# Two-term products of an MLP's up projection: from fp32r parts to scaled f16 parts

## The chip, the core and the metric

The kernel runs on one core of one Trainium2 chip. The metric is device time in microseconds (us): from the start to the end of one execution. Three runs of the kernel before took 3511.21, 3514.76 and 3516.85 us, and its time is their median, 3514.76 us.

The engines are named as in the profile: PE is TensorE (matmuls), PEld its weight loads, DVE is VectorE, ACT is ScalarE, POOL is GpSimd and SP is SyncE, which here only issues DMAs.

## The reference

One layer of a backbone over 2048 latent tokens of width 1024 and 256 context tokens. A projection feeds two mixers side by side, softmax attention (8 query heads, 2 key heads) and a gated delta rule (4 heads, both directions, in chunks of 64). Their outputs are projected and added; then comes a gated MLP with a convolution of width 3 over the positions:

```
x = x + g1 * lat_out
x = x + g2 * conv_ffn(modulate(x, norm2_g, sh2, sc2), w_up, ffn_conv_w, ffn_conv_b, w_down)
return rms_norm(x, final_norm_g)

def modulate(x, g, shift, scale):
    return rms_norm(x, g) * (1.0 + scale) + shift

def conv_ffn(h, w_up, conv_w, conv_b, w_down):
    u = depthwise_conv(h @ w_up, conv_w) + conv_b
    gate, val = jnp.split(u, 2, axis=-1)
    return (jax.nn.silu(gate) * val) @ w_down
```

All of it is float32. `w_up` is 1024 x 5632, `w_down` 2816 x 1024.

## The kernel before, in words

**Products in two parts.** A float32 operand a is kept as a rounded part hi and a rest lo = a - hi. A product of two such operands is three matmuls into one PSUM tile: hi x hi, hi x lo and lo x hi (`prods`, L512 to L521, one line for each). In the projections both parts are fp32r; in the attention both are f16.

**Stages.** Times are those of the profiled execution.

- 0 to 280 us: norm of the input, modulation terms, q, k, v and z projections.
- 280 to 718 us: the delta rule's projections (`pg`), convolution, SiLU (`y`, L1022), normalised k with its decay (`kd`, L966 and L969), written to DRAM as `gsc` (L971). At its end the modulation terms for the MLP are put together (`mod2`, `aff2`, L1063 to L1066).
- 718 to 1780 us: the attention and the delta rule, interleaved (below).
- 1780 to 2027 us: output norms, output projection (`po`), residual, the norm ahead of the MLP. That norm's output h2 goes to DRAM (`h2c`).
- 2027 to 3514 us: the MLP, in four blocks of 512 tokens.

**What sets the order in the attention stage.** The two mixers are recorded as operations of five tracks: `a` (attention), `i0` and `i1` (the part of a chunk of each direction that needs no state), `d0` and `d1` (the part that needs it). A planner (`Plan.order`) gives each operation a duration by a formula, and an urgency by its track's weight, and lays them out engine by engine: on each engine the most urgent operation among those that could start within a short patience is next. The planned order is then issued as it is (`Plan.issue`, L398 to L403, so nearly all instructions of the stage carry L403). Every engine and every DMA queue works through its own list in that order. Tile buffers are rings with a fixed count (`RINGS`): a load into a ring waits until the last reader of the buffer is done.

In the attention a step takes two key chunks for the 4 heads of one key head: four score matmuls `sc`, exp on ACT (`p`), its f16 part `hp` (on DVE for 3 of 9 steps, on ACT for the other 6), the rest `lp` on POOL, and the products with the values (`ops`). There are 288 such steps. For the next group of heads the row maxima are formed ahead, from score tiles `sm` that DVE reduces (`mx`). The scores have one ring of two banks (ring `s` is 1). In the delta rule, `tT`, `tk` and `rows` are loaded for each chunk; `at` is a decay product of the chunk, made in track `i` and used in track `d`.

**The MLP.** For each block there are 44 units of the up projection and then 24 units of the down projection. A unit of the up projection is one block of 1024 x 128 weights: loaded on SP's queue (`fetch`), its hi part cast on ACT (`leading`, L1685), its rest on DVE (`rest`, L1690), 24 matmuls (`pu`). The parts are made two units ahead and the load is asked for four units ahead. `after_up` copies the result from PSUM on ACT (`ue`, L1716), applies the three taps of the convolution on DVE (L1724, L1727; they come from the columns C_FC to C_FB of the constant tile `cols`), and for every second unit forms SiLU(gate) * value in two fp32r parts (`hid`). The next block's h2 is loaded and split while the down projection runs (L1825, L1826).

## Time and profile before

| | |
|---|---|
| median of three runs | 3514.76 us |
| the profiled execution, in all | 3515.73 us |
| its span, first to last instruction | 3513.9 us |
| mean granted clock of TensorE | 0.980 |
| PE busy | 3355.6 us (95%) |
| DVE busy | 2298.6 us (65%) |
| ACT busy | 1639.6 us (47%) |
| POOL busy | 1410.7 us (40%) |
| DMA, whole span | 381.30 MB, mean 109 GB/s |
| `pu` matmuls, three lines | 550.5 + 549.0 + 548.5 us of rows |

The rows of a matmul overlap: a `pu` row lasts 391 ns in the mean, but the next one starts sooner. The pace is therefore read from starts, not from durations, and a busy PE is not a PE at its best pace. An engine's share over the whole span is a mean over stages with different limits; the windows by stage tell which engine is full where. "idle before" in a group is the time that the engine had nothing to do just ahead of those instructions, with what ended it.

### The profile page before, as it was taken

The page shows a single profiled execution, that of the slowest core. Times are in us where ns is not written, and L with a number is a line of the kernel's source. Part 1 is how long each engine was busy: PE and PEld are TensorE (multiplying, and loading weights), DVE is VectorE, ACT ScalarE, POOL GpSimd, SP SyncE. Part 2 cuts the span into 40 slices and gives each one's busy share as a digit, 9 for nine tenths or more (in the row PEclk, how much of TensorE's full clock was granted, in tenths as well). Part 3 has the DMA queues.
Part 4 walks back from the last instruction along what each step waited for, and adds up shares of the span by engine and source line. Part 5 has one row for each costly group of instructions (what it writes and reads, how often), then busy time and mean ns, then how long its engine had stood idle before and what let it go on. Part 6 is the DMA issues. An engine that isn't in the chain of part 4 may idle for free.

```text
span 3513.9 us, 65298 instructions
## 1 busy us (share of the span) xinstructions
PE 3355.6 (95%) x26281; PEld 2715.5 (77%) x26281; DVE 2298.6 (65%) x3619; ACT 1639.6 (47%) x2556; POOL 1410.7 (40%) x1423
## 2 busy tenths in 40 slices
PE   6799999979999999999978999999999999999998
PEld 3799878857777777777756778888888888888898
DVE  5665577887777777777655567735773476447743
ACT  4443233447777676777644443323332333224331
POOL 4684455437767777777765411100110010001100
PEclk7899999989999999999989999999999999999999
DMA  6323335651111222220146643343334333433332
GB/s 227 90 66 97 120 116 149 189 153 48 60 63 55 66 63 70 66 65 29 53 145 218 218 159 96 95 130 112 120 97 124 115 116 97 125 114 120 96 108 91
DMA packets 209199, 381.30 MB, mean 109 GB/s; under 512 B 20360, under 2 KB 95720, under 8 KB 208624
## 3 DMA queue, kind: packets, MB, share of 16 engines
q1 hardware_dynamic: 207056, 371.74, 33.4%
q0 software_dynamic: 1840, 5.39, 0.6%
q8 instruction: 206, 3.38, 0.4%
q14 instruction: 97, 0.79, 0.1%
HBM read 297.73 MB, written 79.72 MB: 107 GB/s over the span
## 4 chain that ended last, share of the span: by engine, by line
PE 77%; DVE 8%; POOL 6%; DMA 4%; issue 3%; ACT 2%; SPq 0%; POOLq 0%; DVEq 0%; ACTq 0%
PE pu L520 9%; PE pu L519 9%; PE pu L521 9%; PE sc L403 6%; PE ops L403 5%; PE pdn L521 5%; PE pdn L520 5%; PE pdn L519 5%; PE po L403 3%; PE sm L403 3%; PE pa L403 1%; PE pg L520 1%; PE pg L519 1%; PE pg L521 1%; PE pkk L403 1%
## 5 line engine op out<-in xcount | busy, mean ns | idle before, releaser
L403 POOL TENSOR_TENSOR lp<-p,hp 128x1024 f16<-128x1024 f32 x288 | 616.0, 2146 | 232.8 <-DVE hp L403 88.0
L519 PE MATMUL pu<-h,ws_u 128*128 128x512 f32 x1408 | 550.5, 391 | 2.8 <-ACT h L403 2.8
L520 PE MATMUL pu<-h,ws_u 128*128 128x512 f32 x1408 | 549.0, 390 | 2.5 <-DVE h L403 2.5
L521 PE MATMUL pu<-h,ws_u 128*128 128x512 f32 x1408 | 548.5, 390 | 0.0
L403 DVE TENSOR_REDUCE mx<-sm 128x1 f32<-128x512 f32 x512 | 336.1, 681 | 74.7 <-PE sm L403 72.6
L1718 POOL COPY carry<-ue 128x2 f32<-128x2 f32 x132 | 24.8, 188 | 891.4 <-ACT ue L1716 891.4
L403 ACT ACTIVATE p<-sc 128x1024 f32<-128x1024 f32 x288 | 294.9, 1024 | 182.7 <-PE sc L403 173.3
L519 PEld LDWEIGHTS pu<-h,ws_u 128*128 128x128 f32 x1408 | 264.7, 188 | 60.1 <-ACT h L403 4.8
L520 PEld LDWEIGHTS pu<-h,ws_u 128*128 128x128 f32 x1408 | 264.6, 188 | 59.6 <-DVE h L403 4.2
L521 PE MATMUL pdn<-hid,ws_d 128*128 128x512 f32 (+2 forms) x880 | 307.4, 349 | 0.0
L520 PE MATMUL pdn<-hid,ws_d 128*128 128x512 f32 (+2 forms) x880 | 307.4, 349 | 0.0
L521 PEld LDWEIGHTS pu<-h,ws_u 128*128 128x128 f32 x1408 | 264.8, 188 | 54.9
L519 PE MATMUL pdn<-hid,ws_d 128*128 128x512 f32 (+2 forms) x880 | 306.4, 348 | 0.0
L1727 DVE SCALAR_TENSOR_TENSOR cv<-ue,cols,cv 128x512 f32<-128x512 f32 (+1 forms) x352 | 264.9, 752 | 15.8 <-DVE cv L1724 0.5
L1716 ACT COPY ue<-pu 128x512 f32<-128x512 f32 x176 | 103.2, 586 | 367.6 <-PE pu L521 367.0
L1690 DVE TENSOR_TENSOR ws_u<-raw_u,ws_u 128x1024 fp32r<-128x1024 f32 x176 | 214.5, 1219 | 19.1 <-ACT ws_u L1685 19.1
L403 PE MATMUL sc<-q,kh 128*128 128x512 f16 x576 | 218.7, 380 | 4.5 <-ACT p L403 3.9
L1724 DVE TENSOR_SCALAR cv<-ue,cols 128x512 f32<-128x512 f32 (+1 forms) x176 | 96.3, 547 | 188.3 <-ACT ue L1716 183.3
L403 PE MATMUL sc<-qx,kx 128*128 128x512 f16 x576 | 218.6, 380 | 0.0
L1715 POOL COPY ue<-carry 128x2 f32<-128x2 f32 x176 | 95.4, 543 | 291.6 <-DVE cv L1727 291.3
L1690 DVE TENSOR_TENSOR ws_d<-raw_d,ws_d 128x1024 fp32r<-128x1024 f32 (+1 forms) x96 | 109.0, 1136 | 157.8 <-ACT ws_d L1685 155.6
L403 ACT CAST hp<-p 128x1024 f16<-128x1024 f32 x192 | 200.8, 1047 | 3.3
(580 smaller groups left out, 8068.1 us busy)
## 6 DMA issues: line engine op xcount, KB each, us to landing
raw_u<-in_wu SPq DMA_DIRECT2D x176, 512.0 KB
raw_d<-in_wd SPq DMA_DIRECT2D x64, 512.0 KB
tk<-gsc SPq DMA_DIRECT2D x34, 512.0 KB
tT<-gsc SPq DMA_DIRECT2D x66, 256.0 KB
wm<-in_wm SPq DMA_DIRECT2D x64, 256.0 KB
gsc<-kd SPq DMA_DIRECT2D x64, 256.0 KB
raw_o<-in_wo SPq DMA_DIRECT2D x32, 512.0 KB
raw_d<-in_wd SPq DMA_DIRECT2D x32, 384.0 KB
```

What stands on the lines that cost most here:

```text
L403: fn(**{k: v.get() if isinstance(v, Lazy) else v for k, v in kw.items()})
L519: PE.matmul(out=ps, lhsT=hi_l(k), rhs=hi_r(k), start=st, stop=False)
L520: PE.matmul(out=ps, lhsT=hi_l(k), rhs=lo_r(k), start=False, stop=False)
L521: PE.matmul(out=ps, lhsT=lo_l(k), rhs=hi_r(k), start=False, stop=en)
L1690: V.tensor_tensor(out=made[u][:, 1, :n], in0=raws[u][:, :n], in1=made[u][:, 0, :n].bitcast(F32), op=ALU.subtract)
L1715: G.tensor_copy(out=ue[:, 0:2], in_=carry[:, b, :])
L1716: S.copy(out=ue[:, 2:514], in_=ps)
L1718: G.tensor_copy(out=carry[:, b, :], in_=ue[:, 512:514])
L1724: V.tensor_scalar(out=cv[:, :W], in0=ue[:, 0:W], scalar1=fw[0], scalar2=cols[:, C_FB + b:C_FB + b + 1], op0=ALU.mult, op1=ALU.add)
L1727: V.scalar_tensor_tensor(out=cv[:, :W], in0=ue[:, i:i + W], scalar=fw[i], in1=cv[:, :W], op0=ALU.mult, op1=ALU.add)
```

## The change

The up projection's two parts become f16. So that f16 holds them, the weights are divided by their overall norm and h2 by a bound on its norm, each times FTOP = 16384; the product of the two scales is divided out of the taps of the convolution. In detail:

- The bound on h2 is formed at the end of the delta rule's projections from `aff2` and `mod2`: five small DVE instructions, a matmul with ones across the partitions, a power on POOL. `aff2` and a copy `sh2` of the shift then carry the scale into h2.
- The norm of the weights is formed beside the attention as a sixth track `n` of the planner, with weight NW = 0.02: each of the 44 weight blocks is loaded once more (`wraw`, two buffers), squared and summed along the row on ACT (`wsq`, `wsum`), then added up on DVE and across the partitions on PE (`wps`).
- Room for it comes from the rings: `tk` goes from 2 buffers to 1, `at` from 1 to 2.
- In the MLP, `leading` scales and rounds in one ACT instruction, `rest` scales and subtracts in one DVE instruction, and the tiles of up-projection weights have a ring of their own. The h2 tiles are f16, half as large.

```diff
-VTOP = 1024.0
+VTOP, FTOP = 1024.0, 16384.0
...
-RINGS = dict(s=1, m=2, o=1, g=3, p=4, hp=4, lp=4, q=2, h=4, fa=1, at=1, fb=2, tT=2, tk=2, st=2, t=2, ti=2, rw=1, fin=1)
-STAG = -0.03
+RINGS = dict(s=1, m=2, o=1, g=3, p=4, hp=4, lp=4, q=2, h=4, fa=1, at=2, fb=2, tT=2, tk=1, st=2, t=2, ti=2, rw=1, fin=1)
+STAG, NW = -0.03, 0.02
...
+        V.scalar_tensor_tensor(out=bsq, in0=aff2, scalar=float(D), in1=aff2, op0=ALU.mult, op1=ALU.mult)
+        V.tensor_tensor(out=bs2, in0=mod2[:, 8:16], in1=mod2[:, 8:16], op=ALU.mult)
+        V.tensor_tensor(out=bsq, in0=bsq, in1=bs2, op=ALU.add)
+        V.tensor_reduce(out=scl[:, 0:1], in_=bsq, axis=AX, op=ALU.add)
+        V.tensor_copy(out=scl[:, 1:2], in_=scl[:, 0:1])
+        PE.matmul(out=ps[:, 0:2], lhsT=ones, rhs=scl[:, 0:2], start=True, stop=True)
+        V.tensor_scalar(out=scl[:, 0:1], in0=ps[:, 0:1], scalar1=2.0, scalar2=1e-30, op0=ALU.mult, op1=ALU.max)
+        G.tensor_tensor(out=scl[:, 0:1], in0=scl[:, 0:1], in1=mhalf, op=ALU.pow)
+        for t, x in ((aff2, aff2), (sh2, mod2[:, 8:16])):
+            V.tensor_scalar(out=t, in0=x, scalar1=scl[:, 0:1], scalar2=FTOP, op0=ALU.mult, op1=ALU.mult)
...
-    plan.issue(dict(a=("work", 1.0), i0=("path", IW), i1=("path", IW, STAG), d0=("path", DW), d1=("path", DW, STAG)))
+    plan.track = "n"
+    sums = plan.tile(ak, [P, 2 * NJ], F32, "wsum", "wsum", 1)
+    for b in range(2 * NJ):
+        raw = plan.tile(ak, [P, KT, P], F32, "wraw", f"wraw_{b}", 2)
+        plan.SY.dma_start(out=raw, in_=wu[b])
+        junk = plan.tile(ak, [P, KT, P], BF16, "wsq", f"wsq_{b}", 1)
+        plan.S.activation(out=junk, in_=raw, func=AF.Square, accum_out=sums[:, b:b + 1])
...
+    plan.PE.matmul(out=wps[:, 0:2], lhsT=ones, rhs=tot, start=True, stop=True)
...
+    plan.issue(dict(n=("work", NW), a=("work", 1.0), i0=("path", IW), i1=("path", IW, STAG), d0=("path", DW), d1=("path", DW, STAG)))
+    G.tensor_tensor(out=scl[:, 1:2], in0=scl[:, 1:2], in1=mhalf, op=ALU.pow)
...
+    V.tensor_scalar(out=cols[:, C_FC:C_FB], in0=cols[:, C_FC:C_FB], scalar1=scl[:, 2:3], scalar2=None, op0=ALU.mult)
...
-                    h2 = mk(hp3, [P, 2, KT, 512], F32R, "h2", "h2_0", 1)
+                    h2 = mk(hp3, [P, 2, KT, 512], F16, "h2", "h2_0", 1)
...
     def leading(u):
+            if how == "u":
+                made[u] = w3.tile([P, 2, 8, P], F16, tag="wh", name=f"ws_{how}{tb}_{b}_{a}", bufs=3)
+                S.activation(out=made[u][:, 0], in_=raws[u], func=AF.Identity, scale=scl[:, 1:2])
+                return
...
     def rest(u):
+            if units[u][0] == "u":
+                V.scalar_tensor_tensor(out=made[u][:, 1], in0=raws[u], scalar=scl[:, 1:2], in1=made[u][:, 0],
+                                       op0=ALU.mult, op1=ALU.subtract)
```

What stands on the engines now, at three places. First ACT's list at the end of the delta rule's projections, before; `y` is the SiLU, `kd` the decayed k, `db` and `lh` the first chunk's work in the attention stage.

```order
L1022 ACTIVATE y_2_8003<-y_2_8003 128x512 [waits DVE_49]
L966 ACTIVATE kd_2_1_8022<-pt_2_8014,beta 128x128 [waits DMAHW6_49,DMAHW3_49,DVE_49]
L966 ACTIVATE kd_2_1_8022<-pt_2_8014,beta 128x128 x3
L1022 ACTIVATE y_3_8009<-y_3_8009 128x512 [waits DVE_49]
L966 ACTIVATE kd_3_1_8036<-pt_3_8028,beta 128x128 [waits DMAHW2_49,DMAHW0_49,DVE_49]
L966 ACTIVATE kd_3_1_8036<-pt_3_8028,beta 128x128 x3
L403 ACT_TABLE_LOAD
L403 ACTIVATE db_0_8188<-pdb_0_8174 128x512 [waits PE_49]
L403 ACTIVATE db_0_8214<-pdb_0_8198 128x512 [waits PE_49]
L403 CAST lh_0_8217<-db_0_8188 128x512 [waits DVE_49]
```

The same place of ACT's list after the change; `wsq` is a Square of a weight block, waiting for its load.

```order
L403 ACTIVATE wsq_8151,wsum<-wraw_8116 128x1024 [waits DMAHW6_49]
L1024 ACTIVATE y_2_8005<-y_2_8005 128x512 [waits DVE_49]
L403 ACTIVATE wsq_8166,wsum<-wraw_8118 128x1024 [waits DMAHW7_49,Activation_49]
L968 ACTIVATE kd_2_1_8024<-pt_2_8016,beta 128x128 [waits DMAHW3_49,DVE_49]
L968 ACTIVATE kd_2_1_8024<-pt_2_8016,beta 128x128 x3
L403 ACTIVATE wsq_8218,wsum<-wraw_8164 128x1024 [waits DMAHW4_49,Activation_49]
L1024 ACTIVATE y_3_8011<-y_3_8011 128x512 [waits DVE_49]
L968 ACTIVATE kd_3_1_8038<-pt_3_8030,beta 128x128 [waits DMAHW2_49,DMAHW0_49,DVE_49]
L968 ACTIVATE kd_3_1_8038<-pt_3_8030,beta 128x128 x3
L403 ACT_TABLE_LOAD
L403 ACTIVATE db_0_8234<-pdb_0_8220 128x512 [waits PE_49]
L403 ACTIVATE wsq_8245,wsum<-wraw_8171 128x1024 [waits DMAHW5_49,Activation_49]
```

A Square stands ahead of each of the last two `y`, one ahead of `kd`, and a fourth ahead of the first `lh`. Second, SP's list of DMAs at the same time, before; `gsc<-kd` are the last writes of the stage that ends.

```order
L403 DMA q_8097<-qsc 128x1024 [waits DMAHW5_49,PE_49]
L403 DMA qx_8132<-qsc 64x1024 [waits DMAHW6_49]
L403 DMA tT_1_8135<-gsc 128x512 [waits DMAHW7_49]
L403 DMA tT_1_8137<-gsc 128x512 [waits DMAHW0_49]
L403 DMA tk_1_8139<-gsc 128x1024 [waits DMAHW1_49,PE_49]
L971 DMA gsc<-kd_1_0_7965 128x4x128 [waits DMAHW2_49,DVE_49]
L403 DMA tk_1_8141<-gsc 128x1024 [waits DMAHW3_49]
L971 DMA gsc<-kd_1_1_7968 128x4x128 [waits DMAHW4_49,Activation_49]
L971 DMA gsc<-kd_2_0_8019 128x4x128 [waits DMAHW5_49,DVE_49]
```

And SP's list there after the change.

```order
L403 DMA q_8112<-qsc 128x1024 [waits DMAHW5_49,PE_49]
L403 DMA wraw_8116<-in_wu 128x1024 [waits DMAHW6_49]
L403 DMA wraw_8118<-in_wu 128x1024 [waits DMAHW7_49]
L403 DMA qx_8154<-qsc 64x1024 [waits DMAHW0_49]
L403 DMA tT_1_8157<-gsc 128x512 [waits DMAHW1_49]
L973 DMA gsc<-kd_1_0_7967 128x4x128 [waits DMAHW2_49,DVE_49]
L973 DMA gsc<-kd_1_1_7970 128x4x128 [waits DMAHW3_49,Activation_49]
L403 DMA wraw_8164<-in_wu 128x1024 [waits DMAHW6_49,DMAHW4_49,Activation_49]
L403 DMA wraw_8171<-in_wu 128x1024 [waits DMAHW7_49,DMAHW5_49,Activation_49]
L403 DMA tT_1_8173<-gsc 128x512 [waits PE_49]
L973 DMA gsc<-kd_2_0_8021 128x4x128 [waits DVE_49]
L973 DMA gsc<-kd_2_1_8024 128x4x128 [waits DMAHW0_49,Activation_49]
```

Four loads of weight blocks have come in, the third and fourth waiting for ACT's Squares, and the two loads of `tk` have gone to a later place. Third, ACT in the middle of the attention, after the change, near the last of the Squares; `t` and `lh` belong to the delta rule, `p` and `hp` to the attention.

```order
L403 ACTIVATE p_0_6_12922<-sc_0_6_12907 128x1024 [waits PE_49,Pool_49]
L403 COPY vn_4_12929<-pv_4_12913 128x512 [waits DMAHW5_49,PE_49]
L403 ACTIVATE wsq_12957,wsum<-wraw_12785 128x1024 [waits DMAHW2_49]
L403 CAST t_5_12410<-pa_0_5_12960 128x2x4x64 [waits PE_49]
L403 ACTIVATE db_5_13001<-pdb_5_12897 128x512 [waits Pool_49]
L403 ACTIVATE p_0_8_13008<-sc_0_8_12977 128x1024 [waits DVE_49,PE_49]
L403 CAST lh_5_13024<-db_5_13001 128x512 [waits DVE_49]
L403 CAST hp_0_8_13041<-p_0_8_13008 128x1024 [waits Activation_49]
L403 ACTIVATE p_0_10_13057<-sc_0_10_13034 128x1024 [waits PE_49]
```

Before, the same steps of attention and delta rule stand on ACT in this way:

```order
L403 CAST lh_5_12761<-db_5_12736 128x512 [waits DVE_49]
L403 COPY o_4_12773<-po_4_12750 128x512 [waits PE_49]
L403 CAST t_5_12406<-pa_0_5_12778 128x2x16x16 [waits PE_49,Activation_49]
L403 ACTIVATE p_0_8_12802<-sc_0_8_12790 128x1024 [waits PE_49]
L403 CAST hp_0_8_12834<-p_0_8_12802 128x1024 [waits Activation_49]
L403 ACTIVATE p_0_10_12848<-sc_0_10_12836 128x1024 [waits PE_49]
```

The Squares lie between the attention's and the delta rule's work, and the two mixers are laid out anew around them. The output stage and the MLP keep their order.

## Rows read from the trace of the kernel before

**Rows 1.** Windows: length; busy us (x count) PE, PEld, DVE, ACT, POOL; PEclk; DMA share; GB/s.

```profile
718.00:757.50 39.50, 23.63 (x196) 14.66 (x197) 31.85 (x55) 14.73 (x31) 5.38 (x5) 0.65 0.65 202
757.50:993.50 236.00, 229.33 (x3270) 174.88 (x3268) 190.50 (x342) 167.77 (x226) 162.23 (x87) 1.00 0.19 58
...
2402.00:2640.00 238.00, 237.47 (x1050) 196.22 (x1049) 173.70 (x234) 94.95 (x137) 24.76 (x87) 1.00 0.34 106
```

**Rows 2.** Timeline of PE, up projection of block 0; start us, duration us, engine, line.

```profile
2269.66 0.39 PE L521 MATMUL pu<-h,ws_u 128*128 128x512 f32 x1
...
2279.18 0.39 PE L521 MATMUL pu<-h,ws_u 128*128 128x512 f32 x1
```

**Rows 3.** Timeline of PE, four score matmuls and the matmul behind them.

```profile
1106.25 0.38 PE L403 MATMUL sc<-q,kh 128*128 128x512 f16 x1
...
1107.11 0.28 PE L403 MATMUL pa<-y,t 128*128 128x64 f16 x4
```

**Rows 4.** Groups by form, weight loads; busy us, mean ns, idle before.

```profile
L519 PEld LDWEIGHTS pu<-h,ws_u 128*128 128x128 f32 x1408 | 264.7, 188 | 60.1 <-ACT h L403 4.8 <-issue 0.7
...
L403 PEld LDWEIGHTS <-kh 128*128 128x128 f16 x576 | 56.1, 97 | 40.6 <-issue 1.4
```

**Rows 5.** Groups by form, passes on ACT and DVE.

```profile
L1690 DVE TENSOR_TENSOR ws_u<-raw_u,ws_u 128x1024 fp32r<-128x1024 f32 x176 | 214.5, 1219 | 19.1 <-ACT ws_u L1685 19.1
...
L1727 DVE SCALAR_TENSOR_TENSOR cv<-ue,cols,cv 128x512 f32<-128x512 f32 x264 | 198.5, 752 | 9.3
...
L1685 ACT CAST ws_u<-raw_u 128x1024 fp32r<-128x1024 f32 x176 | 185.4, 1054 | 23.1 <-PE pdn L521 19.0 <-DMA raw_u<-in_wu 4.1
...
L1734 DVE TENSOR_TENSOR cv<-cv,cv 128x512 f32<-128x512 f32 x66 | 45.2, 685 | 0.0
...
L1736 ACT CAST hid<-cv 128x512 fp32r<-128x512 f32 x66 | 41.0, 621 | 165.4 <-DVE cv L1734 165.4
...
L403 ACT ACTIVATE x<-x,mod 128x512 f32<-128x512 f32 x36 | 24.1, 720 | 6.9 <-DVE x L403 6.6
```

**Rows 6.** Timeline of ACT, a Square with a sum and the next instruction.

```profile
1832.63 0.63 ACT L403 ACTIVATE osq<-oraw 128x512 f32<-128x512 f32 x1 [2.26 <-DMA oraw<-oat]
...
1833.40 0.63 ACT L403 ACTIVATE osg<-oraw 128x512 f32<-128x512 f32 x1
```

**Rows 7.** Groups by form of ACT, 757.5 to 993.5 us.

```profile
L403 ACT ACTIVATE p<-sc 128x1024 f32<-128x1024 f32 x62 | 63.5, 1024 | 38.6 <-PE sc L403 38.3
```

**Rows 8.** Waits of ACT in that stretch; us in total, times, longest.

```profile
ACT p L403 <- PE sc L403: 38.3, 45, 4.1
```

**Rows 9.** Timeline of ACT, the hand-over into the attention.

```profile
728.65 0.63 ACT L1022 ACTIVATE y<-y 128x512 f32<-128x512 f32 x1 [2.12 <-DVE y L1021]
734.86 1.14 ACT L966 ACTIVATE kd<-pt,beta 128x128 f32<-128x128 f32 x4 [5.58 <-DMA gsc<-kd]
736.01 1.28 ACT L403 ACT_TABLE_LOAD   x1
```

**Rows 10.** DMA issues, 700 to 760 us; KB each, median us to landing.

```profile
vraw<-vsc POOLq DMA_DIRECT2D x1, 1152.0 KB, 14.3
tk<-gsc POOLq DMA_DIRECT2D x2, 512.0 KB, 7.8
```

**Rows 11.** Timeline of PE, the hand-over.

```profile
729.33 1.11 PE L958 MATMUL pt<-k,y 128*128 128x128 f32 x4 [8.07 <-ACT y L1022]
```

**Rows 12.** Window of 10 us in the hand-over, columns as in rows 1.

```profile
720.00:730.00 10.00, 1.78 (x7) 1.39 (x8) 8.62 (x10) 1.86 (x6) 1.07 (x1) 0.50 1.05 275
```

**Rows 13.** Timeline of DVE, the hand-over.

```profile
715.46 1.30 DVE L403 COPY y<-i 128x512 f16<-128x512 f16 x6 [2.56 <-PE pg L521]
```

**Rows 14.** Timeline of POOL, the hand-over; each row a DMA's issue.

```profile
711.13 0.63 POOL L403 DMA_DIRECT2D tT<-gsc  x1
...
719.28 1.79 POOL L403 DMA_DIRECT2D vraw<-vsc  x1
```

**Rows 15.** Chain that ended last, in order of time; start us, us, what.

```profile
754.84 1.26 DVE vm L403
```

More of the change, by code (lines that the diff above doesn't have):

```diff
@@ L458 @@
     aff2 = const.tile([P, 8], F32, name="aff2")
+    sh2 = const.tile([P, 8], F32, name="sh2")
+    scl = const.tile([P, 4], F32, name="scl")
     p12 = ExitStack()
@@ L1489 @@
             next(both[d])
-    plan.issue(dict(a=("work", 1.0), i0=("path", IW), i1=("path", IW, STAG), d0=("path", DW), d1=("path", DW, STAG)))
+    plan.track = "n"
[5 more added lines that the diff above has]
+        plan.S.activation(out=junk, in_=raw, func=AF.Square, accum_out=sums[:, b:b + 1])
+    tot = plan.tile(ak, [P, 2], F32, "wtot", "wtot", 1)
+    for i in range(2):
+        plan.V.tensor_reduce(out=tot[:, i:i + 1], in_=sums, axis=AX, op=ALU.add)
+    wps = plan.tile(psa, [P, 512], F32, "g", "wps", RINGS["g"])
+    plan.PE.matmul(out=wps[:, 0:2], lhsT=ones, rhs=tot, start=True, stop=True)
+    plan.V.tensor_scalar(out=scl[:, 1:2], in0=wps[:, 0:1], scalar1=1e-30, scalar2=None, op0=ALU.max)
+    plan.issue(dict(n=("work", NW), a=("work", 1.0), i0=("path", IW), i1=("path", IW, STAG), d0=("path", DW), d1=("path", DW, STAG)))
+    G.tensor_tensor(out=scl[:, 1:2], in0=scl[:, 1:2], in1=mhalf, op=ALU.pow)
+    V.tensor_tensor(out=scl[:, 2:3], in0=scl[:, 0:1], in1=scl[:, 1:2], op=ALU.mult)
+    V.tensor_scalar(out=scl[:, 2:3], in0=scl[:, 2:3], scalar1=FTOP * FTOP, scalar2=None, op0=ALU.mult)
+    V.reciprocal(out=scl[:, 2:3], in_=scl[:, 2:3])
+    V.tensor_scalar(out=scl[:, 1:2], in0=scl[:, 1:2], scalar1=FTOP, scalar2=None, op0=ALU.mult)
+    V.tensor_scalar(out=cols[:, C_FC:C_FB], in0=cols[:, C_FC:C_FB], scalar1=scl[:, 2:3], scalar2=None, op0=ALU.mult)
     p2.close()
@@ L1501 @@
     hp3 = p3.enter_context(tc.tile_pool(name="hp3", bufs=1, side="right", reuse_waits="tile"))
-    def load_h2(pool, tag, bufs, tb):
-        h2 = hp3.tile([P, 2, KT, 512], F32R, tag="h2", name=f"h2_{tb}")
-        for k in range(KT):
-            raw = pool.tile([P, 512], F32, tag=tag, name=f"h2raw_{tb}_{k}", bufs=bufs)
-            SY.dma_start(out=raw, in_=h2c[tb, :, k, :])
-            S.copy(out=h2[:, 0, k, :], in_=raw)
-            V.tensor_tensor(out=h2[:, 1, k, :], in0=raw, in1=h2[:, 0, k, :].bitcast(F32), op=ALU.subtract)
-        return h2
     def output(plan, x3, s3, ol3):
@@ L1689, in rest @@
             n = units[u][4]
-            V.tensor_tensor(out=made[u][:, 1, :n], in0=raws[u][:, :n], in1=made[u][:, 0, :n].bitcast(F32),
-                            op=ALU.subtract)
+            if units[u][0] == "u":
+                V.scalar_tensor_tensor(out=made[u][:, 1], in0=raws[u], scalar=scl[:, 1:2], in1=made[u][:, 0],
+                                       op0=ALU.mult, op1=ALU.subtract)
+            else:
+                V.tensor_tensor(out=made[u][:, 1, :n], in0=raws[u][:, :n], in1=made[u][:, 0, :n].bitcast(F32),
+                                op=ALU.subtract)
             del raws[u]
```

11 lines of the change are left out of this document (7 added, 4 removed).

## The prediction

> **What bounds the kernel now.** I read the page first, then the windows by stage, then the timeline of TensorE (PE) inside two stages, then the groups by form, and last the hand-over into the attention stage. The windows [rows 1] show that PE is the engine that is never free: 229.3 of 236.0 us in a stretch of the attention, 237.5 of 238.0 us in an up projection, both at a granted clock of 1.00 (2.4 GHz). In the up projection VectorE (DVE) is busy 173.7 of those 238.0 us and ScalarE (ACT) 95.0, so there only the pace of the matmuls counts. In the attention ACT has 167.8 of 236.0 us of work and 68 us of rest. Between the two stages, from 718.0 to 757.5 us, PE has 23.6 of 39.5 us at a clock of 0.65.
>
> **The up projection, what goes.** All 4 token blocks together have 4 x 44 x 24 = 4224 matmuls of 128x512. From the first to the last row of [rows 2] are 42 steps (43 rows in a row, none missing) in 9.52 us: 226.7 ns a step in fp32r. The same shape in f16 stands in the attention: four score matmuls, each with weights of its own, take from 1106.25 to 1107.11 us [rows 3], 215 ns a step. So a step gains 11.7 ns; a hundredth of a us in the reading of the four steps is 2.5 ns, so between 9 and 14. 4224 x 11.7 ns = 49.4 us; bounds 38 and 59. A first stretch of some 17 us of block 0, in which the loads set the pace, gains nothing (some 50 steps, 0.6 us), and at the ends of the blocks a little is lost: I take 47 us. The weights now load in a PE instruction of their own, 4224 more in the program; in the trace both kinds have load rows beside the matmuls, 97 ns in f16 against 188 ns [rows 4], below a step's length either way, so I cost them at nothing.
>
> **The up projection, what is added.** The first part of the weights gets a scale per partition. On ACT a 128x512 pass with such an operand takes 720 ns where the cast takes 621 [rows 5], so 1054 becomes about 1154 ns per unit. On DVE the second part becomes a three-operand instruction: 752 against 685 ns at 128x512, so 1219 becomes about 1286 ns. Per unit of 24 x 215 = 5.16 us, DVE then has 173.7/43.8 + 0.07 = 4.04 us and ACT 95.0/43.8 + 0.10 = 2.27 us. Both stay under PE, and the splits run two units ahead (leading and rest are called with u + 2): nothing. If that lead were gone, a unit would wait 0.17 us, 30 us over 176 units. The h2 split only changes its output type, and the down projection, the output stage and all their queues stand as before: 0. The taps of the convolution change in value alone.
>
> **The attention, what is added.** 44 loads of 512 KB on SP's queue, 44 Square passes of 128x1024 with a sum on ACT, one small matmul. A 128x512 Square with a sum holds ACT from 1832.63 to 1833.40 us [rows 6], 0.77 us; the second 512 columns add 1054 - 621 = 433 ns [rows 5]: 1.20 us each, 53 us in all. The order puts the last Square beside the 62nd exp, so all 44 fall into the first quarter: 6 before the first exp and 38 within the next 62. In the trace these 62 exps [rows 7], with the same mix of casts to within five, fill 757.5 to 993.5 us. ACT's load there goes from 167.8 to 167.8 + 38 x 1.20 = 213 us, 90% of the stretch. By the waits, ACT's rest is mostly time for PE's scores: 38.3 us in 45 waits [rows 8], 0.85 us each, less than one Square. So a Square that starts in such a gap ends about 0.35 us too late for the next exp or cast. If half of that reaches PE, 38 x 0.18 = 7 us; I take 8. Bounds: below, -10 (the second buffer of at lets a chunk start before the last is done, and the order as a whole is another one); above, 38 x 1.20 = 46 us, when each Square stands in the chain of score, exp, score. PE has 229.3 of 236.0 us of rows there but waits within them, so half is a choice, nearer to the row of rests (68 us against 46 us needed) than to the upper end.
>
> Square needs its function table in ACT. A table load is in the trace at 736.01 us, 1.28 us [rows 9]; the two programs hold nine each, so no Square brings one: 0. The Trainium skill (ScalarE: Activation LUTs, Table sets) says that a switch between sets costs a load each time; by it 44 Squares between exps could cost 2 x 44 x 1.28 = 113 us, and the count of loads in the order says that this doesn't happen here.
>
> The 38 loads in that stretch are 19.9 MB, 84 GB/s beside the 58 that are there; an up projection moves 106 GB/s at a DMA share of 0.34 [rows 1], so the share stays under one half. What they can do is hold SP: a load waits until the Square two before it is done, and behind it in the queue stand loads of tT, tk, rows and q and the writes of o. These have leads of many us (18 chunks of each direction run in the some 1000 us from 757.5 to 1760, 56 us a chunk); 0 in the middle. With one buffer of tk, a 512 KB load (7.8 us to landing [rows 10]) starts when the chunk before has done its state update; 56 us cover it. Without that cover it would cost 7.8 us a chunk.
>
> **The hand-over into the attention.** Here the added work stands in front of work that is late. PE waits 8.07 us for the SiLU pass y at 728.65 us [rows 9, 11], then starts the first score tiles; ACT waits 5.58 us for a write of gsc until 734.86, since the DMA engines are full (share 1.05 from 720 to 730, PE's clock 0.50) [rows 9, 12]. Now two 512 KB loads stand on SP ahead of the last writes of gsc and two more between them, and on ACT a Square stands ahead of each of the last two SiLUs. Two tk loads of 512 KB, gone from there, pay for two of the four. The first Square can wait some 2 us unseen, since DVE is at other work until the next kd. The third must wait for a load that is issued only when the first Square is done: some 721 us plus a landing of 8 to 14 us (the medians of [rows 10]) is 729 to 735, and y follows at 730 to 736 instead of 728.65. That is 2 to 8 us, and one Square ahead of lh adds 1.2. Some of it is used up by DVE's own work, so I take 4; bounds 0 and 13.
>
> POOL's power for the scale stands between its loads and waits for DVE, which was held by PE until 715.46 [rows 13]. The tT load behind it moves from 711.13 [rows 14] to about 718, the vraw load with it from 719.28 to about 726, plus 14.3 us to landing [rows 10] is 740, needed at 754.84 [rows 15]: 0. If it weren't covered, 6 us; that is in the bound of 13. The last scale products and the taps' product fall into the middle of the attention, six instructions below 0.3 us: 0.
>
> **Sum** against the profiled execution, 3513.9 us span and 3515.7 us in all: 3515.7 - 47 + 8 + 4 = 3480.7. The median of the runs is 1.0 us below that execution, so 3480 us.
>
> **Rivals.**
> (a) The attention costs nothing or gains: 68 us of rest take up 46 us of Squares, and the second at buffer helps. For it: the granted clock of 1.00 and PE's full rows, against it that the gaps are shorter than a Square. 3514.8 - 49 + 2 - 5 = 3463, between 3455 and 3467.
> (b) More of it reaches PE: two thirds of the 46 us, with 6 at the hand-over, 3514.8 - 47 + 31 + 6 = 3505.
> (c) Slower: the Squares stand in the chain of score, exp and score, which has a single pair of banks (ring s is 1). Each pushes the next score by its whole 1.20 us, 44 x 1.20 = 53, and the hand-over costs its 13: 3514.8 - 47 + 53 + 13 = 3534. It decides from the point where more than 47 us of these 66 reach PE. For it: the longest waits of ACT are on PE's scores; against it that PE has other work ready, the value products and the delta rule.
> (d) The change does not speed the matmuls: what holds a step at 226.7 ns is not the type. Then 3514.8 + 12 = 3527. The score rows, with fresh weights at each step, speak against it.
> (e) The weight load sets the pace, and a step falls with it: 226.7 x 97/188 = 117 ns, 4224 x 110 ns = 463 us less, 3065. Against it: the score rows have the 97 ns load and step by 215. The Trainium skill (TensorE: Matmul & The Clock Gate, Back-to-back issue gap) has 131 ns a matmul at 512 columns for streams of load and matmul, which would be 404 us less by its figure; it also has 216 ns for the single gap, and by that the trace agrees.
>
> **Chances.** Forecast (3467 to 3494) 0.55; (a) 0.17; in between and (b) (3494 to 3512) 0.17; (c) 0.07; (d) 0.03; (e) 0.01. The range that holds 8 in 10 is 3460 to 3508. I call it no change within 0.2%, 7 us, about what a measurement of this kernel can tell apart. Faster than 3507.7: 0.55 + 0.17 + 0.01 and most of (b), 0.13: 0.86. Same, 0.06: the end of (b) and the start of (c). Slower, 0.08: the rest of (c) and (d).
>
> **What would show it.** In the profile after: pu steps of 215 to 217 ns and up projections of about 227 us per block instead of 239 or more; DVE's and ACT's passes for ws_u near 1.29 and 1.15 us; 44 Squares of about 1.06 us with a read of the sum behind each, all before some 1000 us; the first exp within 10 us of 757.5 us; the 62nd exp 5 to 20 us later than before; the output stage 247 us long and the down projections as long as before. I am wrong if pu steps stay near 227 ns, if the attention stage is longer by more than 25 us or shorter, or if DVE holds the up projection.

## The result, and the profile after

The changed kernel takes 3489.15 us (median of 5 runs, 3485.88 to 3495.78), the kernel before 3516.85 beside it: a ratio of 0.9923, 95% interval 0.9909 to 0.9938, so 27.7 us less. The forecast was 3480, the range 3460 to 3508. The profiled execution of the changed kernel took 3489.78 us with a span of 3487.7, 26.2 less than the span before. The start times of a few tiles split these 26.2 us by stage:

| stage, by start times in us | before | after | change |
|---|---|---|---|
| last gate projection starts | 715.0 | 708.7 | -6.3 |
| from there to the first score (hand-over) | 41.9 | 49.9 | +8.0 |
| first to last score (attention) | 1017.6 | 1033.2 | +15.6 |
| last score to first up projection (output stage) | 253.0 | 253.1 | +0.1 |
| first up to last down projection (MLP) | 1472.1 | 1428.6 | -43.5 |
| from there to the end | 14.3 | 14.2 | -0.1 |

The two rows of the profiles on which the first three lines rest (median record in ns, first and last start in us), before:

```profile
L403 PE MATMUL sc<-qx,kx x576: 377/379/634, 756.9 to 1774.5; 128*128 128x512 f16 x192
...
L521 PE MATMUL pg<-hl,ws_g x384: 387/389/486, 372.0 to 715.0; 128*128 128x512 f32 x192
```

and after:

```profile
L403 PE MATMUL sc<-qx,kx x576: 377/379/634, 758.6 to 1791.8; 128*128 128x512 f16 x192
...
L523 PE MATMUL pg<-hl,ws_g x384: 387/389/479, 367.2 to 708.7; 128*128 128x512 f32 x192
```

**The MLP.** The changed kernel's windows of the hand-over, of the same 236 us as in [rows 1], and of one up projection (columns as there):

```profile
718.00:757.50 39.50, 21.26 (x128) 11.68 (x129) 25.33 (x44) 13.93 (x30) 3.75 (x4) 0.57 0.62 200
757.50:993.50 236.00, 225.20 (x3225) 170.84 (x3225) 181.74 (x332) 202.58 (x300) 155.07 (x83) 1.00 0.44 137
2409.00:2639.70 230.70, 229.72 (x1068) 104.51 (x1067) 177.32 (x236) 96.46 (x136) 24.66 (x87) 1.00 0.35 108
```

The up projection of a block is 230.7 us long instead of 241.7, and PE is busy in all but one of them; VectorE has 177.3 of 230.7 us. The timeline of PE, the first and the last of 43 rows in a row in the up projection, as in [rows 2]:

```profile
2499.72 0.38 PE L523 MATMUL pu<-h,ws_u 128*128 128x512 f16 x1
...
2508.79 0.38 PE L523 MATMUL pu<-h,ws_u 128*128 128x512 f16 x1
```

42 steps in 9.07 us: 216.0 ns against 226.7. The groups that the change made or lengthened (as in [rows 4, 5]; busy us, mean ns, idle before):

```profile
L1722 DVE SCALAR_TENSOR_TENSOR ws_u<-raw_u,scl,ws_u 128x1024 f16<-128x1024 f32 x176 | 225.1, 1279 | 10.5 <-ACT ws_u L1713 10.5
L1713 ACT ACTIVATE ws_u<-raw_u,scl 128x1024 f16<-128x1024 f32 x176 | 202.2, 1151 | 9.9 <-DMA raw_u<-in_wu 9.9
L521 PEld LDWEIGHTS <-ws_u 128*128 128x128 f16 x1408 | 138.5, 98 | 167.7 <-issue 3.7
L403 ACT ACTIVATE wsq<-wraw 128x1024 bf16<-128x1024 f32 x44 | 46.6, 1059 | 17.8 <-DMA wraw<-in_wu 17.6
L403 ACT ACTIVATION_READ_ACCUMULATOR wsq<-wraw 128x1 f32 x44 | 8.6, 195 | 0.0
```

The two splits take 1279 and 1151 ns, the weight load 98, and a Square with the read of its sum 1059 + 195 ns, 1.25 us.

**The hand-over.** ScalarE's timeline where [rows 9] stand before:

```profile
718.85 1.14 ACT L968 ACTIVATE kd<-pt,beta 128x128 f32<-128x128 f32 x4 [0.48 <-DVE kd L971]
730.48 1.06 ACT L403 ACTIVATE wsq<-wraw 128x1024 bf16<-128x1024 f32 x1 [10.49 <-DMA wraw<-in_wu]
731.45 0.19 ACT L403 ACTIVATION_READ_ACCUMULATOR wsq<-wraw 128x1 f32 x1
731.54 0.61 ACT L1024 ACTIVATE y<-y 128x512 f32<-128x512 f32 x1
```

The third Square waits 10.49 us for its load, and the SiLU y stands behind it. PE's row that answers to [rows 11] waits 15.23 us for y instead of 8.07. On SP's queue (start, us, count) that load was issued at 715.32 us, when the first Square was done:

```profile
715.32 3.42 SPq L403 DMA_DIRECT2D wraw<-in_wu  x2
```

On PE:

```profile
732.21 1.12 PE L960 MATMUL pt<-k,y 128*128 128x128 f32 x4 [15.23 <-ACT y L1024]
```

The chain of waits has the same two steps in it, the load and then y:

```profile
715.32 15.09 DMA wraw<-in_wu
...
731.63 0.53 ACT y L1024
```

Two things were not in the forecast: the gate projections end 6.3 us earlier although nothing in them was edited, and the attention loses nearly twice what was taken for it, in a stretch in which PE's clock is 1.00.

### The profile page after: what moved, and what is told of

The parts are those of the page before. It is cut to its first block, busy times and chain, and to the rows that moved or that the text cites. A ratio compares the mean times of both kernels' runs of the same rounds, so it can differ in the third digit from the quotient of the medians.

```text
span 3487.7 us, 65459 instructions
## 1 busy us (share of the span) xinstructions
PE 3307.2 (95%) x26285; PEld 2330.2 (67%) x26285; DVE 2301.8 (66%) x3635; ACT 1697.3 (49%) x2644; POOL 1416.0 (41%) x1425
## 4 chain that ended last, share of the span: by engine, by line
PE 74%; DVE 9%; POOL 7%; DMA 5%; issue 3%; ACT 2%; SPq 0%; POOLq 0%; DVEq 0%; ACTq 0%
PE pu L522 8%; PE pu L523 8%; PE pu L521 8%; PE sc L403 6%; PE ops L403 5%; PE pdn L523 5%; PE pdn L522 5%; PE pdn L521 5%; PE po L403 3%; PE sm L403 3%; DVE mx L403 1%; PE pa L403 1%; PE pkk L403 1%; PE pg L522 1%; PE pg L523 1%
## 5 line engine op out<-in xcount | busy, mean ns | idle before, releaser
L522 PE MATMUL pu<-h,ws_u 128*128 128x512 f16 x1408 | 535.3, 380 | 3.3 <-DVE h L403 3.2
L521 PE MATMUL pu<-h,ws_u 128*128 128x512 f16 x1408 | 535.3, 380 | 2.1 <-ACT h L403 2.1
L523 PE MATMUL pu<-h,ws_u 128*128 128x512 f16 x1408 | 535.2, 380 | 0.0
L523 PEld LDWEIGHTS <-ws_u 128*128 128x128 f16 x1408 | 138.0, 98 | 171.3 <-issue 6.2
L522 PEld LDWEIGHTS <-ws_u 128*128 128x128 f16 x1408 | 138.0, 98 | 169.5 <-issue 5.3
L521 PEld LDWEIGHTS <-ws_u 128*128 128x128 f16 x1408 | 138.5, 98 | 167.7 <-issue 3.7
L1722 DVE SCALAR_TENSOR_TENSOR ws_u<-raw_u,scl,ws_u 128x1024 f16<-128x1024 f32 x176 | 225.1, 1279 | 10.5 <-ACT ws_u L1713 10.5
L1713 ACT ACTIVATE ws_u<-raw_u,scl 128x1024 f16<-128x1024 f32 x176 | 202.2, 1151 | 9.9 <-DMA raw_u<-in_wu 9.9
```

The costliest lines, as they stand in the source:

```text
L521: PE.matmul(out=ps, lhsT=hi_l(k), rhs=hi_r(k), start=st, stop=False)
L522: PE.matmul(out=ps, lhsT=hi_l(k), rhs=lo_r(k), start=False, stop=False)
L523: PE.matmul(out=ps, lhsT=lo_l(k), rhs=hi_r(k), start=False, stop=en)
L1713: S.activation(out=made[u][:, 0], in_=raws[u], func=AF.Identity, scale=scl[:, 1:2])
L1722: V.scalar_tensor_tensor(out=made[u][:, 1], in0=raws[u], scalar=scl[:, 1:2], in1=made[u][:, 0], op0=ALU.mult, op1=ALU.subtract)
```

## The experiments

### What the attention's cost is made of

Theory 1: ScalarE's time for the Squares pushes the scores. Theory 2: the loads cost, above all at the hand-over. Theory 3: the order that the planner writes around 44 more passes, with its rings, is itself a longer one.

**MLP alone.** The n track is taken out, with a constant for the norm, and the rings are those of before:

```
-    plan.track = "n"   ... 44 loads, Squares, sums, matmul
+    G.memset(scl[:, 1:2], 2048.0)
-RINGS = dict(... at=2, ... tk=1 ...)
+RINGS = dict(... at=1, ... tk=2 ...)
```

> Leaves out the norm of the up projection's weights: no loads and no Squares beside the attention, a constant in place of the norm; f16 parts in the up projection, and the attention's order, rings and instructions word for word those of before. By the start times in the two traces the up projections gave back 43.6 us and the attention with its hand-over took 17.4. All theories: the first output product at 1801.8 us as before, and about 3472 us (3469 to 3476), 0.987 of before. If the up projection's gain leans on the attention's end (another clock, other loads in flight), it falls outside 3466 to 3479.

Measured: 3461.77 us, 0.9856 (0.9842 to 0.9871). Lower than expected: the MLP's length is the changed kernel's (1428.7 us), but the first score starts at 748.7 us, 8 us before that of the kernel before. Most of the reason comes below, with the places of the tiles. Its score rows:

```profile
L403 PE MATMUL sc<-qx,kx x576: 376/379/635, 748.7 to 1768.2; 128*128 128x512 f16 x192
```

**Empty passes.** The changed kernel's order, row for row on every engine, with loads and Squares cut to 16 of 1024 columns as they are issued:

```
+                    if self.ops[i].track == "n" and self.ops[i].eng == "S":
+                        kw = dict(kw, out=kw["out"][:, 0:1, 0:16], in_=kw["in_"][:, 0:1, 0:16])
+                    if self.ops[i].track == "n" and self.ops[i].eng == "SY":
...                      the same for the loads
```

> The changed kernel in its own order of instructions, rings and queues, but each of the 44 loads brings 16 columns of 1024 and each Square passes over those 16: the sum of squares is of a 64th of the weights. What is left of the attention's cost is the order's and the rings'. Theory 1 (ScalarE's time for the Squares pushes the scores): all but 44 short passes is gone, some 3474 us. Theory 2 (the loads hold the hand-over and the queue): also 3474. Theory 3 (the order written for 44 more passes, with one buffer of tk and two of at, is itself the longer one, above all its tail, where the delta rule ends 28 us before the attention instead of 17): 3483 to 3487, with the last score near 1788 us.

Measured: 3473.76 us, 0.9891 (0.9877 to 0.9906). The first score is as early as with the MLP alone, the last one 10 us later; the score rows of its profile, as above:

```profile
L408 PE MATMUL sc<-qx,kx x576: 377/379/635, 748.8 to 1778.3; 128*128 128x512 f16 x192
```

1029.5 us from first to last score, with little work added: theory 3 for the attention itself. The time is the 3474 that theories 1 and 2 gave, but not in their way: the attention is long, and the first score is 10 us earlier. A short Square with the read of its sum still takes 0.41 us, 18 us of ScalarE in all.

**Short passes.** The same with whole loads; only the Squares are cut:

```
+                    if self.ops[i].track == "n" and self.ops[i].eng == "S":
+                        kw = dict(kw, out=kw["out"][:, 0:1, 0:16], in_=kw["in_"][:, 0:1, 0:16])
```

> As the run before it, but the 44 loads are whole (512 KB each): only ScalarE's time for the Squares is gone (16 columns instead of 1024, some 0.4 us with the read of the sum instead of 1.25). Theory 1 (ScalarE's time): as without loads, some 3475 us, 14 us under the changed kernel. Theory 2 (the loads: the third Square's wait at the hand-over, 10.5 us on ScalarE, and contention): no less than 3484, within 5 us of the changed kernel. Theory 3 (order): 3483 to 3487 here and without loads alike.

Measured: 3483.91 us, 0.9917 (0.99 to 0.9933). Its score rows, and ScalarE's timeline around y in the hand-over:

```profile
L406 PE MATMUL sc<-qx,kx x576: 376/379/635, 756.7 to 1786.0; 128*128 128x512 f16 x192
```

In the timeline:

```profile
729.34 0.21 ACT L406 ACTIVATE wsq<-wraw 128x16 bf16<-128x16 f32 x1 [10.32 <-DMA wraw<-in_wu]
...
729.55 0.61 ACT L1027 ACTIVATE y<-y 128x512 f32<-128x512 f32 x1
```

The attention is as long as with empty passes (1029.3 us), but the first score is 8 us later: the whole loads cost at the hand-over and nowhere else, theory 2 there. The third Square, now of 0.21 us, still waits 10.32 us; ScalarE's own time is not what delays y. From here to the changed kernel (1033.2 us) whole Squares add 3.9 us to the attention: that is all that theory 1 is worth, of some 37 us that they add to ScalarE (44 times 1.25 less 0.41 us). Each length here is that of one execution; in the five kernels of this document whose up projection is in fp32r, with the same order in the attention, it is 1017.4 to 1019.5 us, so 2 us are within what executions differ by. And not all of the 3.9 us need be ScalarE's: in the changed kernel's execution PE's granted clock falls to 0.59 for 4 us behind a wait of 2.18 us for VectorE (in that of the short passes, with the same wait, it stays at 1.00), which is 1.2 instead of 2.4 GHz in most of them and some 1.6 us of work (an estimate):

```profile
999.59 0.40 PE L403 MATMUL pt<-i,t 128*128 128x128 f16 x4 [2.18 <-DVE t L403]
```

In the window:

```profile
1000.00:1004.00 4.00, 4.00 (x48) 3.17 (x46) 2.34 (x5) 3.32 (x6) 0.00 (x0) 0.59 0.02 4
```

**Rings alone.** The MLP alone with the changed kernel's rings:

```
-RINGS = dict(... at=1, ... tk=2 ...)
+RINGS = dict(... at=2, ... tk=1 ...)
```

> The first of these runs (no norm, constant scale, f16 up projection), but with the changed kernel's rings: one buffer of tk, two of at; the planner writes its order anew for them. Separates the rings from the 44 passes. Theory 3 in the form that the rings cost: 3480 to 3488, the loads of tk late at some chunks. Theories 1 and 2, or the forecast's zero for one tk buffer: within 3 us of 3472.

Measured: 3463.18 us, 0.9861 (0.9841 to 0.9882); the attention lasts 1020.7 us, against 1019.5 with the rings of before, so the rings cost nothing that can be told from that scatter:

```profile
L403 PE MATMUL sc<-qx,kx x576: 376/379/635, 748.3 to 1769.0; 128*128 128x512 f16 x192
```

Here the delta rule's last product starts at 1728.4 us, 41 us before the last score, so a longer stretch of attention alone at the end, which theory 3 had named, is no cause either.

| us | hand-over | attention | MLP |
|---|---|---|---|
| MLP alone | 39.9 | 1019.5 | 1428.7 |
| + rings | 38.9 | 1020.7 | 1426.0 |
| + order for 44 passes (empty passes) | 39.6 | 1029.5 | 1427.0 |
| + loads (short passes) | 49.0 | 1029.3 | 1428.6 |
| + Squares (the changed kernel) | 49.9 | 1033.2 | 1428.6 |

### Other places for the loads

Theory L: the loads that stand ahead of the hand-over's last writes cost its 9 to 10 us. Theory D: the crowding of the Squares makes the order long. Theory O: any order with 57 us of planned Squares is long.

**Gated.** One edge more for the planner, the rest as in the changed kernel:

```
+    exps = [o.idx for o in plan.ops if o.track == "a" and any(kw.get("func") == AF.Exp for _, kw in o.calls)]
     for b in range(2 * NJ):
+        plan.gate = exps[0]
         plan.SY.dma_start(out=raw, in_=wu[b])
+        plan.gate = None
```

> The changed kernel whole, with one edge more in the planner: no load of the 44 is issued before the first exp's instruction, so that on the queue they stand behind the last writes and the first reads of the hand-over. Theory L (the first loads cost the hand-over 9 to 10 us, by the runs with short and whole loads): the first score at 748 to 750 us instead of 758.3, and 3479 to 3481 if the attention's own length stays 1033. Rival (the loads' 2 x 512 KB only shift the wait: tT and tk come late instead): first score 754 or later, 3486 to 3490.

Measured: 3467.91 us, 0.9866 (0.9852 to 0.9881), against 0.9923 some 20 us under the changed kernel. The score rows of its profile:

```profile
L403 PE MATMUL sc<-qx,kx x576: 377/379/634, 748.7 to 1771.2; 128*128 128x512 f16 x192
```

Its 44 Squares (same columns):

```profile
L403 ACT ACTIVATE wsq<-wraw x44: 1040/1057/1082, 753.2 to 1002.2; 128x1024 bf16<-128x1024 f32 x44
```

And SP's queue in the hand-over (start, length from the first to the last issue of the row):

```profile
710.91 14.66 SPq L973 DMA_DIRECT2D gsc<-kd  x6
...
732.43 22.23 SPq L403 DMA_DIRECT2D wraw<-in_wu  x3
```

The loads now stand behind the hand-over's writes of gsc, and the hand-over takes 40.7 us: theory L holds. The time is 11 us below what was expected, because the attention is shorter too. It lasts 1022.5 us although all 44 Squares still lie in the first quarter, from 753.2 to 1002.2 us. So theories D and O both fall: the crowd of Squares costs no more than 1.8 us over the rings alone, and what was long was the one order that was written with loads and Squares ahead of the first exp. By PE's busy time behind the first score, the empty passes are at 15.4 us after 20 where the rings alone are at 17.6, at 238.6 against 243.9 after 250, at 384.2 against 392.4 after 400, and at 779.5 against 789.1 after 800: it goes in small pieces, 8.2 of the 9.6 us in the first 400. PE's longest waits there (us in total, times, longest) tell for what. In the 400 us behind the first score, rings alone:

```profile
PE pt L403 <- DVE t L403: 2.5, 3, 1.4
...
PE sm L403 <- DVE mx L403: 0.5, 2, 0.3
...
PE sc L403 <- ACT p L403: 0.4, 1, 0.4
```

and with the empty passes:

```profile
PE pt L408 <- DVE t L408: 6.0, 6, 2.2
PE sm L408 <- DVE mx L408: 3.1, 4, 1.6
...
PE sc L408 <- ACT p L408: 1.0, 2, 0.6
```

All rows of the two views together, PE waits 15.0 instead of 7.2 us, 11.8 instead of 6.6 of them for VectorE and 2.4 instead of 0.6 for ScalarE. In the long order it is mostly VectorE's passes, of both mixers, that come late for PE; why they do stays open.

**Spread.** The gated kernel with another edge for each load:

```
-        plan.gate = exps[0]
+        plan.gate = exps[4 + 6 * b]
```

> As the run before it, but load b is tied to exp 4 + 6b, so that the 44 Squares lie over the whole attention (264 exps) instead of the first 62. Theory D (it is the crowding: ScalarE at 87% in the first 240 us, the order planned around it): the attention's scores last 1022 to 1025 us (1020.5 with these rings and no Square), 3469 to 3472 in all. Theory O (any order planned with 57 us of Squares on ScalarE is the longer one, wherever they lie): 1029 to 1034 us, 3478 to 3482. By the theory that ScalarE's time itself costs, the same 3.7 us as in the changed kernel in both.

Measured: 3466.03 us, 0.9858 (0.9843 to 0.9873); attention 1024.2 us (first score at 748.3, last at 1772.5).

**Unplanned.** The spread kernel, with the Squares free of cost for the planner:

```
         plan.S.activation(out=junk, in_=raw, func=AF.Square, accum_out=sums[:, b:b + 1])
+        plan.ops[-1].dur = 0.0
```

> As the run before it, but the planner takes the 44 Squares for free (planned length 0), so that its order is near the one without them and the passes are only put between; on the chip they take their 1.25 us. Theory O: the order is the short one again, 1020.5 us, and ScalarE pushes it by 4 us: 1024 to 1026, 3470 to 3473, some 8 us under the spread one. Theory D: as the spread one, within 3 us. Rival: unplanned passes each hit a pass that the scores wait for: 1032 us or more, 3480 or more.

Measured: 3465.55 us, 0.9856 (0.9842 to 0.9871); attention 1022.0 us (750.8 to 1772.8). Neither differs from the gated one by more than the runs do (their intervals overlap throughout), which again speaks against D and O. All three do the whole work and beat both kernels: 0.986 against 0.9923, intervals apart.

### Why the stages ahead of the change got faster

The change's two constant tiles move all that lies behind them on the left side of the memory by 64 bytes (their 32 and 16 bytes are rounded up to 32 each). In the profiles, the second half of the z projection, 384 steps of 256 columns in fp32r, has a median record of 283 ns before and 276 or 277 in every kernel with the change; by its start times it is 2.4 us shorter. One of its three lines, before and after:

```profile
L559 PE MATMUL pq_z<-ws_z,hl x128: 280/283/365, 324.9 to 371.3; 128*128 128x256 f32 x128
...
L561 PE MATMUL pq_z<-ws_z,hl x128: 276/276/364, 322.4 to 366.5; 128*128 128x256 f32 x128
```

Theory P: the place of the tiles does that.

**64 bytes.** The kernel before, with the two tiles and nothing else:

```
+    sh2 = const.tile([P, 8], F32, name="sh2")
+    scl = const.tile([P, 4], F32, name="scl")
+    G.memset(sh2, 0.0)
+    G.memset(scl, 0.0)
```

> The kernel before, with nothing of the change but its two small constant tiles (48 bytes a partition, zeroed once): every tile that is placed after them moves by 48 bytes. In all five traces of kernels with the change the last gate projection starts at 707.7 to 709.4 us, in the one of before at 715.0, and the steps of the second half of the z projection take 276 instead of 283 ns of record. Theory P (where the tiles lie, or the run of before that was profiled, is not the point of the change): if the place does it, the last gate projection starts near 709 and the time is 3508 to 3510, 0.998 of before. Rival: the profiled execution of before was merely a late one; then 3513 to 3517 and a last gate projection that may start anywhere from 708 to 716. Second rival: the change's other instructions ahead of 715 us (a dozen small ones) do it; then 715 and 3514.

Measured: 3541.49 us, 1.0079 (1.0062 to 1.0096). The first part is as expected, a last gate projection at 706.3 us and a z projection of 276 ns; nobody had expected the second: two small tiles that nothing reads make the kernel 27 us slower. PE's timeline, the first and the last of 43 rows of the up projection:

```profile
2499.79 0.39 PE L523 MATMUL pu<-h,ws_u 128*128 128x512 f32 x1
...
2509.59 0.39 PE L523 MATMUL pu<-h,ws_u 128*128 128x512 f32 x1
```

A step is 233.3 ns instead of 226.7, and the MLP 1501.4 us instead of 1472.1.

**256 and 128 bytes.** One constant tile of that size instead of the two. Theory R: what counts is how the addresses of the weights and of the moving tile lie to each other within 256 bytes.

```
+    moved = const.tile([P, 64], F32, name="moved")   # 256 bytes; [P, 32] for 128
+    G.memset(moved, 0.0)
```

> The kernel before with one constant tile of 256 bytes a partition, zeroed once; everything behind it on the left side of the memory moves by 256 bytes, where the two small tiles of the earlier run moved it by 64 (each is rounded up to 32 bytes) and made the kernel 27 us slower: the step of the up projection's matmuls rose from 226.7 to 233.3 ns, that of the z projection's fell from 120 to 113. Theory R (what counts is how the addresses of a matmul's weights and of its moving tile lie to each other within 256 bytes; the weights stand on the left side, the moving tile on the right): 256 bytes change nothing, steps of 226.7 and 120 ns, 3513 to 3517 us. Rival (an absolute address, or the zeroing itself): steps that differ from before, 3535 or more.

Measured: 3515.7 us, 1.0001 (0.9992 to 1.0011), steps of 226.7 and 120 ns; 43 rows as above, 9.52 us:

```profile
2480.08 0.39 PE L523 MATMUL pu<-h,ws_u 128*128 128x512 f32 x1
...
2489.60 0.39 PE L523 MATMUL pu<-h,ws_u 128*128 128x512 f32 x1
```

So it isn't the tile but its size.

> As the run before it with 128 bytes. Theory R gives no step for this distance; it says that the up projection (weights left, moving tile right) and the z projection may take another step than 226.7 or 233.3 and 120 or 113, while the gate projections, whose two tiles both move, keep 227 to 228 ns, and the down projections their 231.6. If the rise had come from leaving a period of 128 bytes: 226.7 and 120 ns again, 3515.

Measured: 3539.69 us, 1.0064 (1.0047 to 1.0081); the up projection's step is 232.5 ns, the z projection's 118.6. Again the first and the last of 43 rows, 9.76 us for 42 steps:

```profile
2489.02 0.39 PE L522 MATMUL pu<-h,ws_u 128*128 128x512 f32 x1
...
2498.78 0.39 PE L522 MATMUL pu<-h,ws_u 128*128 128x512 f32 x1
```

The gate and the down projections, whose weights and moving tiles both shift, keep 228 and 231.6 ns in all these runs.

**Both moved.** The 64 bytes, and 192 bytes beside h on the other side, so that h lies to its weights as before:

```
+    hq3 = p3.enter_context(tc.tile_pool(name="hq3", bufs=1, side="right"))
+    hq3.tile([P, 48], F32, name="beside")
     hp3 = p3.enter_context(tc.tile_pool(name="hp3", bufs=1, side="right", ...))
```

> The kernel before with the two small constant tiles (left side moved by 64 bytes, as in the run that was 27 us slower) and, in the MLP, 192 bytes beside the moving tile h on the right, so that it lies to its weights as before; nothing else. Theory R (only how the two addresses lie to each other counts): the up projection's step is 226.7 ns again and its 27 us are gone, while the z projections keep their 113 ns and the last gate projection its 706 us: 3505 to 3509, 0.997 to 0.998 of before, without any change in the work. Rival (the absolute place of the weights counts): 233.3 ns and some 3541 us as there.

Measured: 3512.29 us, 0.9997 (0.9988 to 1.0007). The up projection has its step back:

```profile
2499.82 0.39 PE L525 MATMUL pu<-h,ws_u 128*128 128x512 f32 x1
...
2509.34 0.39 PE L525 MATMUL pu<-h,ws_u 128*128 128x512 f32 x1
```

9.52 us for 42 steps, as in [rows 2]; theory R holds for it. The z projection keeps its 276 ns and the last gate projection starts at 708.6 us, but only 1.2 us of that arrive at the end, less than expected and within the interval of no change. The first score starts at 752.2 us here, at 750.2 with 64 bytes, at 754.0 and 755.9 with 256 and 128, and at 748.3 to 750.8 in the kernels with the f16 parts and no early loads; so the place is worth something there, by the kernels without f16 parts 2 to 7 us, but before and 256 bytes, of the same steps, already differ by 3 (756.9 and 754.0). The last gate projection tells the same: it starts at 715.0 and 711.6 us in the two kernels with steps of 120 ns, and at 706.3 to 710.6 (708.6 in the mean) in the eleven with 113.

**Even places.** The spread kernel, with two more moving tiles laid to their weights as h lies to its own in the kernel before:

```
-            hd = hd4.tile([P, 2, 514], F32R, tag="hid", ...)
+            hd = hd4.tile([P, 1088], F32R, tag="hid", ...)   # second part at column 574
+    hd4.tile([P, 48], F32, name="shove")
+        ol3.tile([P, 24], F32, name="shove3", bufs=1)
...      what reads and writes hd by the new columns
```

> The changed kernel with its 44 loads and Squares spread over the attention (3466 us), and two tiles placed anew: the hidden tiles of the down projection get a stride of 4352 bytes and start at the weights' place within 256 bytes (before, a stride of 4112 took them through all places), and the moving tile of the output stage likewise. Theory R: the down projection's step falls from 231.6 to 227 ns in some 1580 steps of 512 columns, 7 us, and perhaps a little in those of 257; the output stage's from 234.2 to 227 in 768, 5 us: 3452 to 3456 us. Rival (the places don't matter there, the step is another thing): 3463 to 3469.

Measured: 3466.01 us, 0.9859 (0.9842 to 0.9877): nothing gained. The output stage's step fell as theory R says, from 234.2 to 227.6 ns in the mean (records from 397 to 389 ns):

```profile
L403 PE MATMUL po<-ol,ws_o x768: 387/389/792, 1802.3 to 2023.4; 128*128 128x512 f32 x192
```

From the first output product to the first up projection it is 221.3 us, where the spread kernel takes 222.2. The stage got only 1 us shorter where the steps alone would give 5, so most of it doesn't hang on PE's pace. The down projection's step barely moved (231.1 from 231.6 ns); its second part starts 8 bytes short of an even place, and whether that spoils it wasn't tried.

## Why the prediction was right, and where not

**Up projection, taken 47 us, measured 43.5.** The mechanism and the pace were right: 216.0 ns (215.9 in the mean over all blocks) where the score rows gave 215, so 10.8 instead of 11.7 ns a step, 45.6 us for 4224. A block came out at 230.7 us where about 227 was forecast, since some 2.5 us beside the steps stay in each, as they did before. The Trainium skill (TensorE: Matmul & The Clock Gate, Back-to-back issue gap) gives 216 ns for the single gap; the trace agrees, and its 131 ns for a stream doesn't appear here. Weight loads of their own cost nothing (98 ns), and the splits came out at 1279 and 1151 ns (1286 and 1154 forecast) and stayed hidden. But the 226.7 ns from which the step was counted turned out to be a property of where the tiles lie: the same work takes 233.3 ns with the changed kernel's constants. Against a kernel before laid out like that, the f16 parts would be worth 1501.4 - 1428.6 = 73 us; against the one before as it is, they are worth the 43.5. That the f16 step is free of such a loss at the place where it lies wasn't known ahead of the run, and other places for it weren't tried.

**Hand-over, taken 4 us, measured 8.0.** The step was named rightly: the third Square waits for a load that is issued when the first is done, and y follows it. y came at 731.54, within the 730 to 736 forecast, but by two misses that cancel: the load was issued at 715.32 instead of some 721, and took 15.09 us instead of 8 to 14. And y would have been free at 722.21 (the MLP alone), not at 728.65, because the stage ahead got faster; so y is 9 us late, and VectorE's own work used up nothing of that, though the prediction counted on it. Against the MLP alone the hand-over is 10.0 us longer. Its bound of 13 held.

**Attention, taken 8 us, measured 15.6.** This is the step that failed, in cause as well as in size. It said that ScalarE is late for the scores because a Square is longer than its rests. ScalarE's load did rise to 202.6 of 236 us, table loads did not come, and the 62nd exp came 12 us late as forecast (5 to 20); but with Squares of 16 columns the attention is as long to within 3.9 us, and with the same Squares in another order it takes 1022.5 us. Nor do PE's scores wait longer for ScalarE: by PE's waits between first and last score it is 3.9 us before and 3.6 after, while waits for VectorE's passes `t` and `mx` grow. Before:

```profile
PE pt L403 <- DVE t L403: 5.1, 8, 1.4
PE sc L403 <- ACT p L403: 3.9, 11, 0.7
...
PE sm L403 <- DVE mx L403: 1.0, 4, 0.3
```

and after:

```profile
PE pt L403 <- DVE t L403: 7.4, 7, 2.2
PE sm L403 <- DVE mx L403: 3.9, 5, 1.6
PE sc L403 <- ACT p L403: 3.6, 8, 0.9
```

Waits for POOL's `lp` fell, from 6.5 to 1.5. PE's idle time in all grew from 23.5 to 30.5 us there; the other 8.6 us are rows of PE, and what lengthens those stays open. In place of the step stand some 9 us for the order itself (with the short passes in it, which by the rate of 3.9 us in 37 would make about 2 of them, an estimate), which the prediction let in only as a possible gain ("the order as a whole is another one"). The order's cost is also not only where it was looked for: by PE's busy time above, 5.3 of 9.6 us are lost by 250 us, where the Squares end, and 4.3 behind them.

**Not in the sum.** The gate projections ended 6.3 us earlier. The constants were costed at nothing; their 64 bytes change the pace of matmuls that no line of the change touches. By the last gate projections of all runs (713.3 us in the mean with steps of 120 ns, 708.6 with 113) that is worth some 5 us, an estimate; the rest can't be told from what executions differ by.

**The sum.** 47 became 43.5, 8 + 4 became 23.6, and 6.3 came as a gift: 26.2 of span against the 35 forecast. That the time lies 9 us from the forecast and not 15 is owed to that gift, which is luck. Of the rivals, (a), an attention for free, is what the gated order nearly gives; (b) and (c), two thirds or all of the Squares' time on PE, are refuted by the short passes, by which it is worth 3.9 us; (d) by the step of 216 ns, and (e) by the same step with a load of 98 ns beside it. Two figures of the prediction are off by its own terms, without weight: a unit of VectorE comes to 4.03 us, and (e) to some 3064.

## What to carry to other kernels

Where a planner writes the order, added side work has a cost of its own that ScalarE's or VectorE's load doesn't show: cut the added instructions to almost nothing in the same order, and what remains is the order's. Keep prefetches out of a hand-over in which late writes fill the queues, by an edge to the first instruction behind it: that one edge was worth some 20 us here, three quarters of what the whole change gained, 9 of them at the hand-over and the rest because the planner's order came out another one. And before a change of type is credited with a faster matmul, move the tiles by 64 bytes: in fp32r the place alone took 27 us.
